# One of a round's two low weight parts moved behind the normalisation in the second attention, and the query's permutation put between transposes and value products

## The chip, the cores and the metric

The kernel runs on one core of one Trainium2 chip. The metric is the device time of the core in microseconds; the time before is 911.38 us, the median of three runs. Five engines work side by side and meet only at semaphores: PE (TensorE) multiplies matrices out of SBUF into PSUM banks, ACT (ScalarE) and DVE (VectorE) work on SBUF and PSUM, POOL (GpSimd) works on SBUF, SP issues the loads of the weights. Each engine takes its own instructions strictly in the order in which they are written.

## The reference

The network has two blocks of two kinds of layers on 256 tokens of 1024 channels; everything is float32. The part that the change touches is the last attention, layer 1 of the second block:

```python
hkv = rms_norm(x, kv_norm_g); kv = (hkv @ w_kv).reshape(B, S, 2, N_KV_HEADS, HEAD_DIM)
k_shared = rope(kv[:, :, 0], cos, sin)
kk, vv = band_blocks(k_shared), band_blocks(kv[:, :, 1])
q = rope((h @ w_q[j]).reshape(B, S, N_Q_HEADS, HEAD_DIM), cos, sin)
m = swa_sink_attention(q, kk, vv, sinks[j]) @ w_o[j]
x = x + rms_norm(m, mix_post_g[layer])
```

There are 16 query heads of 64 channels, 4 key-value heads, a causal window of 128 keys and one sink logit per head in the softmax. The rotation (`rope`) turns a pair x1, x2 of each head into x1 cos - x2 sin and x2 cos + x1 sin. A feed-forward layer with a convolution follows, and ends the program.

## The kernel before

Weights come in 268 chunks of 128 x 1024 numbers (512 KB). Each is loaded by SP into one of four raw buffers (`wraw`), and split exactly into a high and a low part of type float32r: the high part (`whi`, line 130) is a copy on ACT, the low part (`wlo`, line 140) is raw minus high, on DVE unless POOL is named. A product of a split weight with a split operand is three matmuls (line 359). Making a low part also ends the use of its raw buffer, so the load of a later chunk is written right behind each low part (`self.load()` in `low`). `W.highs(n)` writes n high parts and hands back the functions that make their low parts, so that these can be put elsewhere.

The second attention (lines 1230 to 1319) works on pairs of query heads, p0 to p7, in ten rounds of one loop, i = 0 to 9. "Round i" below is one pass of it. In the old text of the loop a round in the middle writes, in this order:

1. `scores2(i)`: eight matmuls (line 1241) into two banks; DVE reads them with mask and sink and takes the maxima (line 1252), and negates these (`nm`, line 1255).
2. `transp2(i - 1)`: six transposes of the weights `p` of the pair before (line 1275), and two copies of them to SBUF on ACT (`pT`, line 1277).
3. `pv2(i - 1)`: the products with the values (line 1285), then `split_out`: the high part `oh` on ACT (line 328) and the low part `ol` on DVE (line 329).
4. `rope_fin("q{i + 2}")`, in rounds 0 to 5: the rotation of a later query. PE multiplies the query `f` (a piece of the tile `scr`) with a permutation matrix (line 1168); DVE multiplies that with the sines (line 1170); POOL multiplies `f` with the cosines (line 1171) and adds the two (line 1172).
5. `lows`: the low parts of the chunks whose high parts the round before made. That is one in rounds 1 and 7, two in rounds 2 to 6.
6. `exps2(i)`: the exponentials on ACT (lines 1264 and 1266), which wait for `nm`; then `normalise(i)` on DVE: the sums (`sm`, line 682), their reciprocals (line 684) and four products (line 688).
7. `W.highs(2)`: up to two high parts on ACT.
8. `next(q_fill)`, in rounds 0 to 4: half a unit of the projection of query i + 3, 24 matmuls (line 359), copied to `scr` by ACT (line 1163). From round 5 on it is `wo_t0`, matmuls of the output projection.

So PE's order in a round is scores, transposes, value products, permutation, 24 matmuls. Nothing but this order and the waits on data and buffers decides when something runs. The banks for scores, value products, permutation and projection are taken from four in turn (`bank()`), five per round in rounds 1 to 4.

Of the kernel before, what the change touches and what calls it, by code (L numbers as in the profile page):

```python
# [24 lines left out]

# [1 line left out]
C_QA, C_KA, C_QB, C_KB, C_VB, C_GA, C_GB = 0, 4, 8, 12, 13, 14, 22  # L27
# [8 lines left out]

# [1 line left out]
(V_G0, V_B0, V_BOUT, V_G1, V_B1, V_BFF2, V_G2, V_B2, V_MIXPRE0, V_PSCALE, V_MIXPOST0, V_FFNPRE0,  # L38
 V_FFNPOST0, V_KVG, V_MIXPRE1, V_MIXPOST1, V_FFNPRE1, V_FFNPOST1, V_VAB, V_SINK) = range(20)

# [1 line left out]
W_POOL = 114  # L42
W_KVQ = W_POOL + 2 + 66
W_KV_AT = (0, 1, 4, 5)

# [1 line left out]
K_ID = 0  # L47
# [27 lines left out]
class Weights:  # L75
    """Streams the weight chunks: load, then an exact split w = hi + lo into two float32r parts."""

# [27 lines left out]
    def prepare(self, n=99):  # L105
        """The work on loaded chunks that goes ahead of their split."""
        while n and self.todo:
            n -= 1
            i = self.todo.pop(0)
            self.before[i](self.raw[i])  # L110
# [6 lines left out]
    def high(self):  # L117
        """The high part of the next chunk; returns what makes the low part."""
        i, r = self.split, self.raw.pop(self.split)
        while i in self.todo:  # L120
            self.prepare(1)
        slot = self.slots.pop(0)
        pool, tag = slot
        hi = pool.tile([P, 1024], F32R, tag=tag + "h", name="whi", bufs=1)
        lo = pool.tile([P, 1024], F32R, tag=tag + "l", name="wlo", bufs=1)
        for j, g in enumerate(self.gain.get(i, [])):
            d = slice(j * T, (j + 1) * T)
            self.nc.scalar.activation(out=hi[:, d], in_=r[:, d], func=AF.Identity, scale=g)
        if i not in self.gain:
            self.nc.scalar.activation(out=hi, in_=r, func=AF.Copy)  # L130
        self.ready[i] = (hi, lo, slot)
        self.split += 1

        def low(eng=None):
            for j, g in enumerate(self.gain.get(i, [])):
                d = slice(j * T, (j + 1) * T)
                self.nc.vector.scalar_tensor_tensor(out=lo[:, d], in0=r[:, d], scalar=g, in1=hi[:, d].bitcast(F32),
                                                    op0=ALU.mult, op1=ALU.subtract)
            if i not in self.gain:
                (eng or self.nc.vector).tensor_tensor(out=lo, in0=r, in1=hi.bitcast(F32), op=ALU.subtract)  # L140
            self.done += 1
            self.load()
        return low
# [4 lines left out]
    def take(self, k, c):  # L148
        """The next chunk, its two parts seen as [128, k, c]."""
        if self.taken not in self.ready:  # L150
            self.pump(1)
        hi, lo, slot = self.ready.pop(self.taken)
        self.taken += 1
        self.held.append(slot)
        return tuple(t.rearrange("p (k c) -> p k c", k=k) for t in (hi, lo)) + (slot,)
# [7 lines left out]
    def extra(self, ctx):  # L163
        """One more slot, until its pool is closed."""
        self.grow(ctx, 1)
        return self.slots[-1]
# [10 lines left out]
def model(tc, x_in, wts, bvec, cols_in, const_in, nab_in, pos_in, out):  # L177
    nc = tc.nc
    from contextlib import ExitStack
    with ExitStack() as top:  # L180
# [6 lines left out]
        def rot(pool, shape, dt, tag, name, bufs):  # L187
            """A tile of the next of bufs slots, in turn."""
            key = (id(pool), tag)
# [39 lines left out]
        class Spread:  # L229
            """A row on all partitions, in two banks."""  # L230

# [20 lines left out]

# [1 line left out]
        def rstd_of(v):  # L254
# [4 lines left out]
        def ln_rstd(st):  # L259
            """Mean and 1 / sqrt(var + eps) from the two halves' statistics."""  # L260
            mv = small([P, 2], "mv")
# [28 lines left out]
        def sq_half(src, junk, ss, q, into=None):  # L290
            """ss[:, q] = the half's sum of squares / 1024."""
            nc.scalar.activation(out=junk[:, HALF[q if into is None else into]], in_=src, func=AF.Square, scale=1.0 / 32.0,
                                 accum_out=ss[:, q:q + 1])
# [37 lines left out]
        def fm_banks(h):  # L331
            """[128 tokens, 1024] transposed into two banks."""
            bs = []
# [13 lines left out]
        def to_fm(h, xt, t):  # L347
            """Token tile t of h [128 tokens, 1024] into the split transposed operand."""
            fm_split(fm_banks(h), xt, t)
# [4 lines left out]
        def mm3(o, w, x, start, stop, w_stat):  # L354
            """o += w.x over the split parts; w_stat: the weights are the stationary operand."""
            pairs = ((0, 0), (0, 1), (1, 0))
# [4 lines left out]
        def unit_a(kx, epi, nk=8, pump=(2, None), ahead=0):  # L361
            """Two outputs [128 features, 256 tokens] of a product with stationary weights."""
            cs = [W.take(4, 256) for _ in range(nk // 4)]
# [16 lines left out]
        def unit_halves(kx, epi):  # L380
            """unit_a, one output at a time."""
            cs = [W.take(4, 256) for _ in range(2)]
# [13 lines left out]
        class Tm:  # L396
            """First units of a product with token-major outputs, so that token tile 0 can run alone."""

# [5 lines left out]
            def run(self, t, quiet=(), late=None):  # L404
                """late: what the last unit is to be followed by, emitted ahead of its last products."""
                for u in range(self.n):
# [26 lines left out]
        class Acc:  # L433
            """Token-major product accumulated over the chunks: out [256 tokens, 1024] in four banks."""

# [20 lines left out]
            def tail(self, kxs, chain0, mid, pre=0, post=3, at=(2, 2), half=lambda: None, halves=True, fills=()):  # L456
                """The last chunks: token tile 0 first, then tile 1 while chain0 runs."""
                k0 = self.nk - len(kxs)
# [21 lines left out]

# [1 line left out]
        xT = new_xt(com)  # L482
# [71 lines left out]

# [1 line left out]
        va = apool.tile([P, 2, 512], F32, name="va")  # L556
# [216 lines left out]

# [1 line left out]
        ctx_x.close()  # L775
# [22 lines left out]

# [1 line left out]
        mag = float(1.5 * 2 ** 23)  # L800
# [65 lines left out]

# [1 line left out]
        ctx_f = ExitStack()  # L868
# [43 lines left out]

# [1 line left out]
        dT = new_xt(com)  # L914
# [21 lines left out]
        def a_scale(t, r):  # L936
            """The rms factors of the tokens into the rows of the pooling matrix."""
            for a in [pa[t]] + [corner] * (t == 0):
# [9 lines left out]
        def pool_corner():  # L948
            """What the last tokens of tile 0 give to the first ones of tile 1."""
            b = bank()  # L950
# [47 lines left out]
        def resid_rms(halves, t, gpost, junk):  # L998
            """X += rms_norm(halves) * gpost."""
            ss = small([P, 2], "ss")  # L1000
# [58 lines left out]

# [1 line left out]
        def conv_ffn(layer, xt, second, gpost_row, chain_t, after, split):  # L1061
# [86 lines left out]

# [1 line left out]
        assert W.gone(extra)  # L1150
# [79 lines left out]
        def bank_ahead(n):  # L1230
            """One of the banks that the second token tile takes at the end."""
            i = (turn[id(ps), "b"] + 1 + n) % 4
# [65 lines left out]
        for i in range(10):  # L1298
            if i < 8:
                scores2(i)  # L1300
            if 1 <= i <= 8:
                transp2(i - 1)
                split_out(pv2(i - 1), *att2[i - 1])
            if i < 6:
                rope_fin(f"q{i + 2}")
            for low in lows:
                low()
            if i < 8:
                exps2(i)
                normalise(i, lambda a, j: a[:, j * P:(1 + 2 * j) * P])  # L1310
            lows = W.highs(2)
            if i == 0:
# [43 lines left out]
def fm_unit(w):  # L1356
    """[K, 256] -> chunks [128, 4 * 256]."""
    k = w.shape[0] // 128
# [3 lines left out]
def tm_chunks(w):  # L1362
    """[K, N] -> chunks of [128, 1024 / N row blocks, N]."""
    k, n = w.shape[0] // 128, w.shape[1]
# [106 lines left out]
def lay_na_bias(rpb):  # L1471
    """[8, 15, 31] -> [4, 128, 2, 384]: per query column and row parity, the offsets of six key rows."""
    flat = np.concatenate([rpb.reshape(8, -1), np.full((8, 1), NEG, np.float32)], 1)
# [35 lines left out]
```

## Time and profile before

| what | us |
|---|---|
| three runs | 908.84, 912.42, 911.38 |
| median | 911.38 |
| span of the profiled execution, first to last instruction | 908.3 |
| second attention, loop rounds 1 to 8, first transpose to last `oh` | 638.6 to 692.8 |
| PE, DVE, ACT, POOL busy over the span | 859.9, 631.5, 493.0, 242.6 |

No time of the profiled execution is known besides its span; the shortest of the three runs is 0.5 us above it. Busy times say how long an engine held instructions, and what bounds a stretch is read from the waits in that stretch. A wait in a timeline stands in brackets, with the engine and the tile that ended it. PE's ends are modelled, so the place where the next PE instruction starts is the better mark.

### The profile page before, as it was taken

To read this page: it belongs to the slowest core of one execution; us is meant where nothing else is said; L and a number is where in the kernel's file an instruction comes from. 1 tells how busy PE (TensorE), PEld (TensorE's weight loads), DVE (VectorE), ACT (ScalarE), POOL (GpSimd) and SP (SyncE) were. 2 spreads that over 40 slices of the span, in tenths; PEclk is the share of its full clock that TensorE was granted. 3 is DMA by queue.
4 is the path that set the end of the run, shared out by engine and by line. 5 is a ranking of instruction groups with operands and counts; after the bars stand their busy time and mean duration, and the time that the engine had idled before them with its cause. 6 is when DMAs were issued, how large, how long until landed. Compare 5 with 4: busy or idle time off the path is not lost.

```text
span 908.3 us, 15197 instructions
## 1 busy us (share of the span) xinstructions
PE 859.9 (95%) x5872; PEld 771.2 (85%) x5872; DVE 631.5 (70%) x1019; ACT 493.0 (54%) x905; POOL 242.6 (27%) x196
## 2 busy tenths in 40 slices
PE   6999999889899999989999999999889899999997
PEld 5988899779698999779999999989666898999995
DVE  5466754877738755777789777665786678977762
ACT  4555755433526645354657545555775466754551
POOL 4161040324998000353240000138631223000000
PEclk9999999989899999999999999999999999999999
DMA  8683354346526855623547555433252454755431
GB/s 307 203 275 125 117 186 138 118 136 233 193 94 217 294 187 186 208 71 115 186 152 248 205 200 172 162 119 125 94 155 101 141 184 166 253 208 187 174 127 46
DMA packets 43897, 154.61 MB, mean 170 GB/s; under 512 B 5009, under 2 KB 5905, under 8 KB 43826
## 3 DMA queue, kind: packets, MB, share of 16 engines
q1 hardware_dynamic: 41616, 146.90, 47.8%
q0 software_dynamic: 1632, 5.93, 2.0%
q8 instruction: 46, 0.75, 0.3%
q10 hardware_dynamic: 578, 0.82, 0.3%
q14 instruction: 25, 0.20, 0.1%
HBM read 152.58 MB, written 1.05 MB: 169 GB/s over the span
## 4 chain that ended last, share of the span: by engine, by line
PE 68%; DVE 12%; issue 6%; ACT 5%; DMA 5%; POOL 2%; SPq 0%; DVEq 0%; POOLq 0%; ACTq 0%
PE bank_a L359 35%; PE bank_b L359 22%; PE bank_a L414 5%; DVE wlo L140 4%; DMA wraw<-wts_dram 3%; ACT whi L130 2%; DMA nab<-nab_dram 1%; PE bank_a L1285 1%; PE bank_a L710 1%; POOL wlo L140 1%; PE bank_b L699 1%; DVE X L321 1%; PE bank_b L647 1%; DMA v<-bvec_dram 1%; POOL wraw L845 1%
## 5 line engine op out<-in xcount | busy, mean ns | idle before, releaser
L140 DVE TENSOR_TENSOR wlo<-wraw,whi 128x1024 fp32r<-128x1024 f32 x225 | 288.8, 1313 | 81.2 <-ACT whi L130 75.2
L359 PE MATMUL bank_a<-xh,whi 128*128 128x256 f32 x1056 | 299.6, 284 | 5.0 <-DVE cv L1075 5.0
L359 PE MATMUL bank_a<-xh,wlo 128*128 128x256 f32 x1056 | 296.1, 280 | 0.8 <-POOL wlo L140 0.4
L359 PE MATMUL bank_a<-xl,whi 128*128 128x256 f32 x1056 | 295.9, 280 | 0.0
L130 ACT ACTIVATE whi<-wraw 128x1024 fp32r<-128x1024 f32 x261 | 265.1, 1049 | 40.3 <-DMA wraw<-wts_dram 33.9
L359 PEld LDWEIGHTS bank_a<-xh,whi 128*128 128x128 f32 x1056 | 199.3, 189 | 10.2 <-ACT whi L130 6.5
L359 PEld LDWEIGHTS bank_a<-xl,whi 128*128 128x128 f32 x1056 | 199.4, 189 | 1.9
L359 PEld LDWEIGHTS bank_a<-xh,wlo 128*128 128x128 f32 x1056 | 199.3, 189 | 1.4 <-DVE wlo L140 0.8
L140 POOL TENSOR_TENSOR wlo<-wraw,whi 128x1024 fp32r<-128x1024 f32 x36 | 93.6, 2613 | 175.6 <-ACT whi L130 87.5
L1072 ACT ACTIVATE cv<-bank_a,cols 128x256 f32<-128x256 f32 x76 | 41.9, 558 | 85.7 <-PE bank_a L359 85.7
L256 POOL TENSOR_TENSOR rstd<-ve,neghalf 128x1 f32<-128x1 f32 x22 | 13.4, 611 | 233.8 <-DVE ve L297 192.1
L1073 DVE SCALAR_TENSOR_TENSOR cv<-bank_a,cols,cv 128x255 f32<-128x255 f32 x76 | 36.5, 481 | 50.2 <-ACT cv L1072 49.9
L359 PE MATMUL bank_b<-wlo,ah 128*128 128x512 f32 x176 | 69.5, 395 | 0.0
L359 PE MATMUL bank_b<-whi,al 128*128 128x512 f32 x176 | 69.3, 394 | 0.0
L359 PE MATMUL bank_b<-whi,ah 128*128 128x512 f32 x176 | 69.3, 394 | 0.0
L856 POOL TENSOR_SCALAR wraw<-wraw,cols 128x256 f32<-128x256 f32 x28 | 30.2, 1094 | 125.9 <-DMA wraw<-wts_dram 122.7
L359 PE MATMUL bank_b<-whi,uh 128*128 128x512 f32 x128 | 51.5, 402 | 4.3 <-ACT uh L328 4.3
L359 PE MATMUL bank_b<-whi,ul 128*128 128x512 f32 x128 | 51.5, 402 | 1.7 <-DVE ul L329 1.7
L359 PE MATMUL bank_b<-wlo,uh 128*128 128x512 f32 x128 | 51.5, 402 | 0.0
L359 PEld LDWEIGHTS bank_b<-wlo,ah 128*128 128x128 f32 x176 | 33.1, 188 | 7.6
L359 PEld LDWEIGHTS bank_b<-whi,ah 128*128 128x128 f32 x176 | 33.1, 188 | 6.3
L1075 DVE SCALAR_TENSOR_TENSOR cv<-bank_a,cols,cv 128x254 f32<-128x254 f32 x76 | 36.6, 482 | 2.7
(201 smaller groups left out, 1371.3 us busy)
## 6 DMA issues: line engine op xcount, KB each, us to landing
wraw<-wts_dram SPq DMA_DIRECT2D x268, 512.0 KB, 4.5
v<-bvec_dram POOLq DMA_DIRECT2D x10, 512.0 KB, 6.7
v<-bvec_dram SPq DMA_DIRECT2D x4, 512.0 KB, 7.1
nab<-nab_dram SPq DMA_DIRECT2D x4, 384.0 KB, 6.3
poolA<-const_dram POOLq DMA_DIRECT2D x1, 544.0 KB, 6.1
scr<-x_dram SPq DMA_DIRECT2D x2, 256.0 KB, 3.1
scr<-x_dram SPq DMA_DIRECT2D x1, 512.0 KB, 10.3
out_dram<-X SPq DMA_DIRECT2D x2, 256.0 KB, 2.1
```

The costliest lines, as they stand in the source:

```text
L130: self.nc.scalar.activation(out=hi, in_=r, func=AF.Copy)
L140: (eng or self.nc.vector).tensor_tensor(out=lo, in0=r, in1=hi.bitcast(F32), op=ALU.subtract)
L256: nc.gpsimd.tensor_tensor(out=r, in0=v, in1=neghalf, op=ALU.pow)
L321: nc.vector.scalar_tensor_tensor(out=x[:, s], in0=junk[:, s], scalar=r, in1=x[:, s], op0=ALU.mult, op1=ALU.add)
L359: nc.tensor.matmul(o, lhsT=l, rhs=r, start=start and i == 0, stop=stop and i == 2)
L414: nc.tensor.matmul(o[:, :256], lhsT=self.kx(k)[b][:, t * P:(t + 1) * P], rhs=self.cs[u][k // 4][a][:, k % 4, :], start=i == 0 and k == 0, ...
L647: nc.tensor.matmul(s[e][:, j * T:(j + 1) * T], lhsT=q[r, j * P:(j + 1) * P], rhs=k[r, :], start=True, stop=True)
L699: nc.tensor.transpose(out=b[:, s * T + j * P:s * T + (j + 1) * P], in_=pt[e][:, j, s * P:(s + 1) * P], identity=ident)
L856: nc.gpsimd.tensor_scalar(out=d, in0=d, scalar1=g, scalar2=None, op0=ALU.mult)
L1072: nc.scalar.activation(out=v, in_=o[:, :T], func=AF.Identity, scale=col(c + 2), bias=col(c + 3))
L1073: nc.vector.scalar_tensor_tensor(out=v[:, 1:T], in0=o[:, 0:T - 1], scalar=col(c + 1), in1=v[:, 1:T], op0=ALU.mult, op1=ALU.add)
L1075: nc.vector.scalar_tensor_tensor(out=v[:, 2:T], in0=o[:, 0:T - 2], scalar=col(c), in1=v[:, 2:T], op0=ALU.mult, op1=ALU.add)
```

## The change

In the loop of the second attention two things are written in another place. The permutation of a query (`rope_fin`) now stands between the transposes and the value products of a round. And of a round's low parts the first stays ahead of the exponentials and the normalisation, while the second, where there is one, comes behind them. The rest of the diff takes comments and docstrings away.

```diff
             if 1 <= i <= 8:
                 transp2(i - 1)
-                split_out(pv2(i - 1), *att2[i - 1])
             if i < 6:
                 rope_fin(f"q{i + 2}")
-            for low in lows:
+            if 1 <= i <= 8:
+                split_out(pv2(i - 1), *att2[i - 1])
+            for low in lows[:1]:
                 low()
             if i < 8:
                 exps2(i)
                 normalise(i, lambda a, j: a[:, j * P:(1 + 2 * j) * P])
+            for low in lows[1:]:
+                low()
             lows = W.highs(2)
```

On PE, in round 2 (rows with + are new there, rows with - are gone; `bank_t` takes the transposes):

```order
 L1241 MATMUL bank_a<-k_6876,q_6894 128x256 x2
 L1275 MATMUL bank_t<-ident,p 128x128 x6
+L1168 MATMUL bank_a<-scr,perm_6631 128x256
 L1285 MATMUL bank_a<-pT,v_6635 64x256 x2
 L1285 MATMUL bank_a<-pT,v_6635 64x128 x2
-L1168 MATMUL bank_a<-scr,perm_6631 128x256
 L359 MATMUL bank_a<-xh,whi 128x256
 L359 MATMUL bank_a<-xl,whi 128x256
```

The permutation moved from behind the value products to ahead of them; rounds 1 to 5 have this. On DVE, in round 3 before, from the negated maxima to the first score operation of the next round:

```order
L1255 TENSOR_SCALAR nm<-mx 128x4
L329 TENSOR_TENSOR ol<-bank_a,oh 128x256
L1170 TENSOR_TENSOR q_7232<-bank_a,sin_2272 128x256
L140 TENSOR_TENSOR wlo<-wraw,whi 128x1024 x2
L682 TENSOR_TENSOR sm<-sm,es 128x4
L684 RECIPROCAL rc<-sm 128x4
L688 TENSOR_SCALAR p<-p,rc 128x128
L688 TENSOR_SCALAR p<-p,rc 128x256
L688 TENSOR_SCALAR p<-p,rc 128x128
L688 TENSOR_SCALAR p<-p,rc 128x256
L1252 ISA p,mx<-bank_a,l1m,sink 128x128
```

And the same stretch of DVE after:

```order
L1255 TENSOR_SCALAR nm<-mx 128x4
L1170 TENSOR_TENSOR q_7223<-bank_a,sin_2272 128x256
L329 TENSOR_TENSOR ol<-bank_a,oh 128x256
L140 TENSOR_TENSOR wlo<-wraw,whi 128x1024
L682 TENSOR_TENSOR sm<-sm,es 128x4
L684 RECIPROCAL rc<-sm 128x4
L688 TENSOR_SCALAR p<-p,rc 128x128
L688 TENSOR_SCALAR p<-p,rc 128x256
L688 TENSOR_SCALAR p<-p,rc 128x128
L688 TENSOR_SCALAR p<-p,rc 128x256
L140 TENSOR_TENSOR wlo<-wraw,whi 128x1024
L1252 ISA p,mx<-bank_a,l1m,sink 128x128
```

The sine product went ahead of `ol`, and one low part behind the normalisation, ahead of the next round's score operations. Rounds 2 to 6 have the second; the order of ACT, POOL and SP is the same in both, but SP's load behind the second low part now waits for it in its new place.

## Rows read from the trace of the kernel before

**Rows 1.** Chain of waits, 646 to 693 us, shares by line.

```profile
by line: DVE wlo L140 26.3%; PE bank_a L1285 17.9%; PE bank_t L1275 10.1%; ACT pT L1277 8.5%; PE bank_b L359 7.7%; DVE p L688 6.4%; issue 5.3%; ACT oh L328 4.1%; ACT p L1264 3.7%; DVE q L1170 2.7%; DVE ol L329 2.4%; DVE rc L684 2.0%; PE ban
```

**Rows 2.** Windows, one round each: length; PE, PEld, DVE, ACT, POOL busy; clock.

```profile
646.30:654.18 7.88, 7.01 (x50) 5.11 (x49) 6.87 (x19) 6.07 (x18) 2.93 (x3) 1.00 0.23 62
654.18:661.79 7.61, 6.84 (x49) 5.18 (x49) 6.61 (x20) 5.62 (x16) 2.35 (x2) 1.00 0.47 142
669.39:677.38 7.99, 6.96 (x37) 4.46 (x37) 6.71 (x20) 5.38 (x15) 3.46 (x4) 1.00 0.44 139
677.38:683.85 6.47, 6.22 (x35) 4.04 (x35) 5.47 (x19) 4.41 (x14) 0.00 (x0) 1.00 0.89 298
683.85:689.85 6.00, 5.37 (x27) 3.52 (x27) 4.43 (x18) 3.46 (x13) 0.00 (x0) 1.00 0.45 157
```

**Rows 3.** Timeline of PE: start, duration (us), instruction, count, idle time before it.

```profile
646.30 0.55 PE L1275 MATMUL bank_t<-ident,p 128*128 128x128 f32 x3
...
654.18 1.16 PE L1275 MATMUL bank_t<-ident,p 128*128 128x128 f32 x6 [0.64 <-DVE p L688]
...
655.52 1.32 PE L1285 MATMUL bank_a<-pT,v 128*64 128x256 f32 x8 [0.18 <-ACT pT L1277]
...
656.77 0.70 PE L1168 MATMUL bank_a<-scr,perm 128*128 128x256 f32 x2
...
657.12 0.47 PE L359 MATMUL bank_a<-xh,whi 128*128 128x256 f32 x1
...
660.28 0.93 PE L1241 MATMUL bank_a<-k,q 64*128 64x128 f32 x8
```

**Rows 4.** Timeline of DVE, round 3, and two rows from other rounds.

```profile
645.00 2.23 DVE L688 TENSOR_SCALAR p<-p,rc 128x128 f32<-128x128 f32 x4
...
654.76 0.35 DVE L1252 CUSTOM_DVE_ANT_0 p<-bank_a,l1m,sink 128x128 f32<-128x128 f32 x1
...
656.23 0.17 DVE L1255 TENSOR_SCALAR nm<-mx 128x4 f32<-128x4 f32 x1
...
657.30 0.42 DVE L329 TENSOR_TENSOR ol<-bank_a,oh 128x256 fp32r<-128x256 f32 x1 [0.90 <-ACT oh L328]
...
657.97 3.16 DVE L140 TENSOR_TENSOR wlo<-wraw,whi 128x1024 fp32r<-128x1024 f32 x2
...
661.05 0.15 DVE L682 TENSOR_TENSOR sm<-sm,es 128x4 f32<-128x4 f32 x1
...
661.45 1.01 DVE L688 TENSOR_SCALAR p<-p,rc 128x128 f32<-128x128 f32 x4
...
680.74 2.35 DVE L140 TENSOR_TENSOR wlo<-wraw,whi 128x1024 fp32r<-128x1024 f32 x2
```

**Rows 5.** Timeline of POOL, a rotary add alone, and one beside two lows.

```profile
631.07 0.74 POOL L1172 TENSOR_TENSOR q<-q,scr 128x256 f32<-128x256 f32 x1
...
658.44 1.60 POOL L1172 TENSOR_TENSOR q<-q,scr 128x256 f32<-128x256 f32 x1
```

**Rows 6.** Timeline of ACT, round 3 to the next.

```profile
656.88 0.38 ACT L328 ACTIVATE oh<-bank_a 128x256 fp32r<-128x256 f32 x1 [0.95 <-PE bank_a L1285]
...
657.16 0.39 ACT L1264 ACTIVATE p<-p,nm 128x128 f32<-128x128 f32 x1
...
659.29 1.99 ACT L130 ACTIVATE whi<-wraw 128x1024 fp32r<-128x1024 f32 x2
...
661.19 0.36 ACT L1163 ACTIVATE scr<-bank_a 128x256 f32<-128x256 f32 x1
...
662.58 0.95 ACT L1277 ACTIVATE pT<-bank_t 128x384 f32<-128x384 f32 x2 [1.03 <-PE bank_t L1275]
...
664.49 0.38 ACT L328 ACTIVATE oh<-bank_a 128x256 fp32r<-128x256 f32 x1 [0.95 <-PE bank_a L1285]
```

**Rows 7.** DMA issues, 630 to 712 us: count, KB each, us to landing.

```profile
wraw<-wts_dram SPq DMA_DIRECT2D x18, 512.0 KB, 3.7
v<-bvec_dram POOLq DMA_DIRECT2D x2, 512.0 KB, 6.8
```

## The prediction

> **What bounds the kernel now.** I read the chain of waits of the second attention first [rows 1]: the low parts on DVE are its largest item, 26.3%, ahead of the value products on PE (17.9%) and the transposes (10.1%), so DVE's order in a round sets PE's pace. The windows [rows 2], each from a round's first transpose to the next round's, show rounds of 7.88, 7.61 and 7.99 us with POOL at work (a further one of 7.60 lies between), then 6.47 and 6.00 once POOL is idle. The granted clock is 1.00, the upper of its two levels (2.4 GHz), throughout.
>
> PE's timeline [rows 3] has two stalls per round: 0.64 us for the first normalised weights (DVE's `p`), 0.18 us for the first copy `pT`. DVE [rows 4] shows why. It idles 0.90 us until `oh` comes, because `ol` stands first; then come `ol`, the sine product and both lows, and only then the sums: 657.30 to 661.05. The exponentials were done at 659.29, when ACT began its high parts [rows 6]: the normalisation stands 1.76 us behind its data. A second thing sits inside that: two lows alone take 2.35 us, here 3.16 [rows 4], and POOL's rotary add takes 1.60 beside them, 0.74 alone [rows 5].
>
> The Trainium skill (SBUF — State Buffer, section Who interferes with whom) explains the last rows by a pair of ports that DVE and POOL lock against each other for a whole instruction, whoever starts first; two SBUF inputs take it, one PSUM input does not. The rows agree: 3.16 - 2.35 = 0.81 is lost on one side and 0.86 on the other, and `ol` keeps its 0.42. By that rule alone nothing is saved by merely shifting POOL's add, since the first low would wait it out (up to 0.74); by stretching in proportion it would lose less. Neither changes the sum below, where that low has slack, but the rule makes the fourth rival.
>
> **The second low behind the normalisation** (rounds 2 to 6, five instructions moved, none added). DVE's way from `ol` to the sums loses one low, about 1.2 us (half of 2.35), and then ends with the exponentials. The sums start about 1.8 us sooner against their round. What is late next must be found by adding up each engine's loop, with the permutation already ahead.
>
> - PE: transposes 0.55 for three [rows 3], that is about 0.8 for six when nothing paces them (now 1.16, since `p` comes piece by piece over 1.01); permutation 0.35 (657.12 - 656.77); value products 1.25 (656.77 - 655.52); 24 matmuls 3.16 (660.28 - 657.12); scores 0.86 to 0.93. Sum 6.4 to 6.5.
> - ACT [rows 6]: `oh` 0.28 (to 657.16), exponentials 2.13, two highs 1.90, `scr` up to 0.36, two copies 0.95, and 0.96 from the copies' end (663.53) to the next `oh` (664.49). Sum 6.5 to 6.6.
> - DVE, as a loop with ACT: exponentials 2.13, sums and reciprocals 0.40, four products 1.01, the second low 1.17, score operations 1.47 (656.23 - 654.76), `nm` 0.17, and the exponentials again. With 0.1 of handing over, 6.4 to 6.5.
>
> All three lie within 0.2 us of each other, at about 6.5 against 7.61. That is the gain of a regular round, 1.1 us, and it leaves no cover: each tenth that any of the three loses is a tenth of the round. The lower bound of a round is PE's sum without the copies' pacing, 6.2; the upper is 7.0, if hand-overs and POOL put 0.5 on the DVE loop. I take 6.5, which the undisturbed round of 6.47 also shows possible [rows 2].
>
> **The permutation ahead of the value products** (rounds 1 to 5, one PE instruction pair, one DVE product and, through them, two POOL instructions). On PE it fills 0.35 us in which the copies `pT` run: the wait of 0.18 goes, and the value products find both copies ready sooner. `scr`, which it reads, must be there: in the new steady round ACT makes it just ahead of the copies, so it does not come later than they do. `oh` would come up to 0.17 later; the wait that goes pays for it. On DVE the sine product slides into the 0.90 us in which DVE waits for `oh`, at no cost. POOL's cosine product (0.74) then falls beside the score operations, which read PSUM, and its add ahead of the first low instead of between the two lows. I cost a late add at 0.5 us on the first low, hidden because the exponentials end later than that low. It is already contained in the 6.5; alone, this move would give some 0.2 to 0.3 per round on PE.
>
> **The load behind the second low** starts about 0.8 us later in its round (sums 1.76 sooner, but sums, products and the low itself, 0.40 + 1.01 + 1.17, now ahead of it) while the rounds get shorter. It is wanted by the second high of the next round, which comes after score operations, `nm`, exponentials and one high: 1.47 + 0.17 + 2.13 + 0.95, with 0.1 of handing over 4.8 us. Landing takes 3.7 [rows 7]: cover of 1.1 us, and no cost.
>
> **The sum**, round by round. Round 1 has one low and POOL is busy with earlier work, so it keeps its time. Round 2's window, 7.88, gets 6.8, since its `p` (2.23, beside POOL [rows 4]) still hold its transposes: -1.1. Two rounds of 7.61 and 7.60 get 6.5: -2.2. The round of 7.99 has the permutation but half of an output projection (PE 3.08) in place of the 24 matmuls, no `scr`, and the next has no copy pending: 6.4, -1.6. The round of 6.47 loses only what paces its transposes, -0.3 (from 0 to -0.4). The last, 6.00, waited for nothing but `oh` and the exponentials; now the second low ahead of its score operations holds `nm` back: +0.3 (0 to +0.4). Total -4.9, by bounds: regular rounds at 6.2 would give -5.8 (three times 0.3 more), at 7.0 -2.5 (rival 1). I take 0.2 off for hand-overs at three equal loops: -4.7. What follows the attention starts from its last value products: the shift is handed on whole, because the later loads are written behind later lows and shift too.
>
> The profiled execution is known by its span, 908.3 us; the run nearest to it took 908.84, the median 911.38 lies 3.1 above the span. Nothing in the edit scales with that, so I subtract from the median: 911.4 - 4.7 = 906.7 us.
>
> **Rivals.**
>
> 1. *DVE becomes the bound.* The score operations now stand behind a low; with 0.5 us of hand-overs and POOL's add, rounds last 7.0 (the first of them 7.3), the round of 7.99 gets 6.9, and the last two lose 0.4 together: -0.6 x 3 - 1.1 + 0.4 = -2.5, 908.9 us. For it: DVE's loop has 0.1 of slack. Against it: DVE is busy only 6.61 of 7.61, 0.81 of that being time lost beside POOL.
> 2. *The second load comes late.* At 6.0 us rather than 3.7 the second high waits 1.2, and `scr`, the permutation and `pT` behind it on ACT. Rounds 3 to 5 have such a high: 3.6 given back, 910.3 us. For it: the vector loads, which run beside the weights, take 6.8 for 512 KB [rows 7]. Against it: loads in these rounds come singly now, and less than half of the DMA time is used in three of the windows.
> 3. *Taken back later.* The feed-forward after the attention waits for a load; if that ended on something that does not move, 911.4 us. Against it: that load is written behind a low part which waits for this attention's end.
> 4. *Slower: POOL locks the normalisation.* If POOL's add comes after the first low has begun, it waits for the low and then falls on the four products, which take 2.23 instead of 1.01 beside POOL [rows 4]. The place is the DVE loop; each low there can meet a POOL product too, at the 0.6 that the second of a pair loses at most (3.16 - 2.35 = 0.81 over both): 6.5 + 1.2 + 0.6 + 0.6 = 8.9 per round against 7.88, 7.61, 7.60 and 7.99 (+1.0, +1.3, +1.3, +0.9), and +0.8 in the last two rounds: +5.3, 916.7 us. It decides from the point where the sine product comes later than `oh`; by the timeline `nm` ends 0.5 us before `oh` begins (656.40, 656.88). The Trainium skill's rule of the lock, named above, would put POOL's add there.
> 5. *More than forecast.* With both copies ready the value products run their two halves side by side, the rounds come to 6.2: -5.8, 905.6 us. For it: PE's loop is the shortest of the three. Against it: ACT's 6.5 then still holds.
>
> That the change doesn't do what it says is excluded by the order of instructions, but for round 1.
>
> **How the numbers follow.** Chances: forecast 0.60, rivals 0.14, 0.05, 0.05, 0.07 and 0.09. A measurement of this kernel tells 0.5%, 4.6 us, from no change, and the forecast of -4.7 sits on that bound. It holds 0.38 of its 0.60 for faster, with rival 5: 0.47. Within 0.5%: the forecast's other 0.22, rivals 1 to 3, 0.02 of rival 4: 0.48. Slower: the other 0.05 of rival 4. The likeliest case alone is 905.4 to 908.0; the range takes in rivals 1, 2 and 5 and the runs' own scatter of about a microsecond: 904.0 to 910.3.
>
> **What would show it.** Right: rounds from transpose to transpose of 6.4 to 6.6; no PE wait for `p` in rounds 3 to 6; DVE's sums right behind the exponentials' end; the sine product ahead of `ol`, inside the wait for `oh`; POOL's add back near 0.74 and the first low below 1.8 us; ACT as the engine without idle time. Wrong: a wait of the second high for its load (rival 2), exponentials waiting for `nm` in regular rounds (rival 1), products of over 2 us (rival 4), or a longer wait for weights in the feed-forward.

## The result, and the profile after

The changed kernel takes 906.65 us, the median of eight runs (903.89 to 907.66), against 911.31 us for the kernel before, eight runs (908.84 to 917.01) beside it. The ratio is 0.9948, with an interval of 95% from 0.9929 to 0.9967: faster, by 4.7 us or 0.5%, and on which side of 0.5% the interval leaves open. The forecast was 906.7 us, 4.7 less than the median of three runs that was known then.

The profiled execution of the changed kernel took 905.71 us. Its page begins:

```profile
span 903.9 us, 15201 instructions
...
PE 855.5 (95%) x5872; PEld 770.0 (85%) x5872; DVE 632.4 (70%) x1019; ACT 492.1 (54%) x905; POOL 238.7 (26%) x196
```

The span is 4.4 us shorter than before. Every run of the changed kernel is listed 1.8 us above its span (905.71 and 903.9), so the span of 908.3 us before answers to some 910.1 us, an estimate, and not to the run of 908.84 us that the prediction took as the nearest. Comparing the same instructions in both traces: the first transposes of round 1 start 0.94 us later than before (639.50 against 638.56), with nothing changed ahead of them; then 5.1 us are won between the first transposes of round 2 and those of round 8; what comes after is shifted as a whole (the last transposes by -4.11, the last instruction by -4.4). The start of round 1 lies anywhere from 635.9 to 639.9 us in the ten traces of this case. So the stretch "round 2 to round 8" is used below as the measure: 43.54 us before, 38.47 after. It is read from one execution each, but rounds 3 and 4 agree within 0.01 us in both traces (7.61 and 7.60, 6.42 twice).

The windows of the changed kernel, one round each, from first transpose to first transpose (columns: length; PE, PEld, DVE, ACT and POOL busy, with counts; granted clock; DMA share; GB/s):

```profile
647.26:653.97 6.71, 6.43 (x50) 5.02 (x48) 5.74 (x20) 5.11 (x17) 2.07 (x3) 1.00 0.17 45
653.97:660.39 6.42, 6.31 (x50) 5.11 (x48) 6.30 (x20) 5.47 (x17) 1.47 (x2) 1.00 0.55 166
666.81:673.26 6.45, 6.34 (x39) 4.36 (x37) 6.32 (x20) 5.50 (x17) 2.59 (x4) 1.00 0.56 204
673.26:679.46 6.20, 5.89 (x36) 4.04 (x34) 5.34 (x18) 5.09 (x15) 0.00 (x0) 1.00 0.88 311
679.46:685.73 6.27, 5.15 (x28) 3.53 (x27) 5.32 (x18) 3.50 (x13) 0.00 (x0) 1.00 0.51 164
```

These answer to [rows 2], line by line: 7.88, 7.61, 7.99, 6.47 and 6.00 became 6.71, 6.42, 6.45, 6.20 and 6.27. (The round from 660.39, not shown, is another one of 6.42.) The clock was at its upper level in both.

PE in round 3 (start, duration in us, instruction, count; idle time before it would stand in brackets), against [rows 3]:

```profile
653.97 0.87 PE L1275 MATMUL bank_t<-ident,p 128*128 128x128 f32 x6
654.96 0.70 PE L1168 MATMUL bank_a<-scr,perm 128*128 128x256 f32 x2
655.59 0.98 PE L1285 MATMUL bank_a<-pT,v 128*64 128x256 f32 x8
...
660.39 0.87 PE L1275 MATMUL bank_t<-ident,p 128*128 128x128 f32 x6
```

No wait stands in brackets here: the 0.64 us for `p` and the 0.18 us for `pT` are gone, six transposes take 0.87 instead of 1.16 since each piece of `p` lies ready when it is wanted, and the value products 0.98 instead of 1.32. PE is not free of ACT, though. The loads of its weights (PEld), which go ahead of the matmuls, wait for `scr` and for the copies `pT`:

```profile
654.96 0.30 PEld L1168 LDWEIGHTS bank_a<-scr,perm 128*128 128x128 f32 x2 [0.35 <-ACT scr L1163]
655.59 0.74 PEld L1285 LDWEIGHTS bank_a<-pT,v 128*64 128x64 f32 x8 [0.33 <-ACT pT L1277]
```

DVE in the same round, against [rows 4]:

```profile
656.71 0.17 DVE L1255 TENSOR_SCALAR nm<-mx 128x4 f32<-128x4 f32 x1
656.79 0.42 DVE L1170 TENSOR_TENSOR q<-bank_a,sin 128x256 f32<-128x256 f32 x1
657.13 0.41 DVE L329 TENSOR_TENSOR ol<-bank_a,oh 128x256 fp32r<-128x256 f32 x1
657.46 1.72 DVE L140 TENSOR_TENSOR wlo<-wraw,whi 128x1024 fp32r<-128x1024 f32 x1
659.19 0.16 DVE L682 TENSOR_TENSOR sm<-sm,es 128x4 f32<-128x4 f32 x1
...
659.60 1.01 DVE L688 TENSOR_SCALAR p<-p,rc 128x128 f32<-128x128 f32 x4
660.53 1.22 DVE L140 TENSOR_TENSOR wlo<-wraw,whi 128x1024 fp32r<-128x1024 f32 x1
661.66 0.34 DVE L1252 CUSTOM_DVE_ANT_0 p<-bank_a,l1m,sink 128x128 f32<-128x128 f32 x1
...
663.13 0.17 DVE L1255 TENSOR_SCALAR nm<-mx 128x4 f32<-128x4 f32 x1
```

From `nm` on DVE has no gap. The 0.90 us in which it had idled for `oh` are gone: the second low now stands ahead of the score operations, so `nm` ends at 656.88, when `oh` (656.61, below) is already running. The sine product and `ol` follow, and the sums come at 659.19. One low is 1.72 us long, the other, behind the products, 1.22. POOL's add, against [rows 5], is back at its time alone, and ACT, against [rows 6], has ended its exponentials 0.1 us ahead of the sums:

```profile
655.74 0.73 POOL L1171 TENSOR_TENSOR scr<-scr,cos 128x256 f32<-128x256 f32 x1 [4.56 <-PE bank_a L1168]
657.35 0.74 POOL L1172 TENSOR_TENSOR q<-q,scr 128x256 f32<-128x256 f32 x1 [0.88 <-DVE q L1170]
```

```profile
656.61 0.39 ACT L328 ACTIVATE oh<-bank_a 128x256 fp32r<-128x256 f32 x1 [0.95 <-PE bank_a L1285]
656.92 0.41 ACT L1264 ACTIVATE p<-p,nm 128x128 f32<-128x128 f32 x1
...
659.06 1.99 ACT L130 ACTIVATE whi<-wraw 128x1024 fp32r<-128x1024 f32 x2
660.96 0.36 ACT L1163 ACTIVATE scr<-bank_a 128x256 f32<-128x256 f32 x1
...
663.02 0.38 ACT L328 ACTIVATE oh<-bank_a 128x256 fp32r<-128x256 f32 x1 [0.95 <-PE bank_a L1285]
663.34 0.40 ACT L1264 ACTIVATE p<-p,nm 128x128 f32<-128x128 f32 x1
```

The sums had stood 1.76 us behind the exponentials. The second high (659.06, two in one row) waits for no load. In the chain of waits (shares by line, 647 to 690 us) the lows have fallen from the first place, 26.3% [rows 1], to 5.3%. The exponentials lead, and value products, high parts and permutation, which follow them by way of ACT and PE, hold 12.2, 11.6 and 5.9%:

```profile
by line: ACT p L1264 25.2%; PE bank_a L1285 12.2%; ACT whi L130 11.6%; DVE p L688 8.9%; DVE p L1252 6.1%; PE bank_a L1168 5.9%; DVE wlo L140 5.3%; ACT es L1266 5.3%; PE bank_b L359 4.3%; issue 3.8%; ACT oh L328 3.6%; PE bank_t L1275 2.9%; A
```

### The profile page after: what moved, and what is told of

It reads as the page before. It is cut to its first block, busy times and chain, and to the rows that moved or that the text cites. A ratio compares the mean times of both kernels' runs of the same rounds, so it can differ in the third digit from the quotient of the medians.

```text
span 903.9 us, 15201 instructions
## 1 busy us (share of the span) xinstructions
PE 855.5 (95%) x5872; PEld 770.0 (85%) x5872; DVE 632.4 (70%) x1019; ACT 492.1 (54%) x905; POOL 238.7 (26%) x196
## 3 DMA queue, kind: packets, MB, share of 16 engines
HBM read 152.58 MB, written 1.05 MB: 170 GB/s over the span
## 4 chain that ended last, share of the span: by engine, by line
PE 68%; DVE 10%; issue 8%; ACT 6%; DMA 5%; POOL 3%; SPq 0%; POOLq 0%; DVEq 0%; ACTq 0%
PE bank_a L359 36%; PE bank_b L359 22%; PE bank_a L414 4%; DMA wraw<-wts_dram 3%; DVE wlo L140 3%; ACT whi L130 2%; POOL wlo L140 2%; ACT p L1264 2%; PE bank_a L710 1%; PE bank_b L699 1%; DVE X L321 1%; DMA v<-bvec_dram 1%; PE bank_b L647 1%; DMA nab<-nab_dram 1%; DVE p L688 1%
```

## The experiments

Each kernel's result is given as the lengths of its rounds, from the first transposes of round 2 on, and their sum. "Rounds" are those of 7.88, 7.61, 7.60, 7.99, 6.47 and 6.00 us in the kernel before (43.54) and of 6.71, 6.42, 6.42, 6.45, 6.20 and 6.27 in the changed one (38.47). Edits are shown against the changed kernel, unless said otherwise. Ratios are to the kernel before; where none is given, one execution was read. The intervals of most of these ratios overlap, so the shares rest on the rounds, from one execution of each kernel; rounds that an edit leaves alone come out the same within 0.01 us (6.47 and 5.99 or 6.00 in four of the kernels). Theory A, the prediction's own, books most of the gain on the second low.

**The permutation alone.** Both lows back ahead of the normalisation.

```diff
-            for low in lows[:1]:
+            for low in lows:
                 low()
...
-            for low in lows[1:]:
-                low()
```

> The permutation between transposes and value products as in the changed kernel, both low parts ahead of the normalisation as before. Measure: from the first transposes of round 2 to those of round 8, 43.55 us before, 38.47 us changed. Theory A (the prediction's shares): the second low behind the normalisation is what pays, the permutation alone gives 0.2 to 0.3 us a round on PE: 42.4 to 42.8 us, regular rounds 7.3 to 7.4, time 0.1% under before. Theory B (either part alone pays nearly all): the permutation alone takes POOL's add from between the lows (0.8 us) and the sine product from behind oh (0.4 us), so the sums stand 0.5 instead of 1.8 us behind the exponentials, which PE's own work covers: 38.3 to 39.2 us, regular rounds 6.5 to 6.6, time ratio to before about 0.995.

Rounds of 6.87, 6.53, 6.51, 6.75, 6.47 and 5.99: 39.12 us, 4.4 of the 5.1 us. The time is 907.11 us, ratio 0.9959 [0.9942, 0.9976]. Theory A falls. DVE and POOL in round 3 of it (columns as above):

```profile
655.79 0.41 DVE L1170 TENSOR_TENSOR q<-bank_a,sin 128x256 f32<-128x256 f32 x1
656.55 0.42 DVE L329 TENSOR_TENSOR ol<-bank_a,oh 128x256 fp32r<-128x256 f32 x1 [0.35 <-ACT oh L328]
656.89 2.41 DVE L140 TENSOR_TENSOR wlo<-wraw,whi 128x1024 fp32r<-128x1024 f32 x2
```

```profile
656.34 0.74 POOL L1172 TENSOR_TENSOR q<-q,scr 128x256 f32<-128x256 f32 x1 [0.49 <-DVE q L1170]
```

The sine product fills part of DVE's wait for `oh`, the add follows right behind it and is over (657.08) 0.2 us after the lows begin, and the pair of lows takes 2.41 us instead of 3.16.

**The second low alone.** The permutation back behind the value products.

```diff
+            if 1 <= i <= 8:
+                split_out(pv2(i - 1), *att2[i - 1])
             if i < 6:
                 rope_fin(f"q{i + 2}")
-            if 1 <= i <= 8:
-                split_out(pv2(i - 1), *att2[i - 1])
```

> The second low part behind the normalisation as in the changed kernel, the permutation behind the value products as before. Same measure. Theory A: 39.3 to 39.8 us, that is the changed kernel's 38.47 plus what the permutation gave on PE. Theory B: 38.8 to 39.3 us, regular rounds 6.6 to 6.75; so the two parts' gains would not add up (each about 4.5 us alone, 5.1 together). Theory C (the second low in the loop from exponentials over scores to exponentials costs what it saves unless the sine product goes ahead): 42 us or more.

Rounds of 7.14, 6.70, 6.69, 6.87, 6.19 and 6.33: 39.93 us, 3.6 us won. The time is 908.47 us, ratio 0.9952 [0.9931, 0.9973]. That is just above theory A's 39.8, 0.6 above theory B's range and well under theory C's 42. With the first experiment: 4.4 and 3.6 alone, 5.1 together, so the gains don't add up, and each part by itself takes most of what DVE's late sums cost. What is left differs. With the permutation alone PE's own work sets the round: it is busy 6.47 of 6.52 us, and the chain of waits runs on PE without a break from 653.53 to 673.31. With the second low alone it is DVE and ACT. POOL's add begins after the first low here (658.21, 1.48 us long), runs on when that is over, and holds the sums back, which take 0.39, 0.45 and 0.65 us in rounds 3 to 5 instead of 0.16. That is the prediction's fourth rival on a small scale:

```profile
658.68 1.60 POOL L1172 TENSOR_TENSOR q<-q,scr 128x256 f32<-128x256 f32 x1
```

```profile
659.91 0.39 DVE L682 TENSOR_TENSOR sm<-sm,es 128x4 f32<-128x4 f32 x1 [0.23 <-ACT es L1266]
```

**PE's order alone.** The permutation is early on PE, but DVE's order is the old one, `oh`'s low part ahead of the sine product, and both lows ahead of the normalisation.

```diff
-            if i < 6:
-                rope_fin(f"q{i + 2}")
+            rest = rope_fin(f"q{i + 2}", True) if i < 6 else None
             if 1 <= i <= 8:
                 split_out(pv2(i - 1), *att2[i - 1])
+            if rest:
+                rest()
...
```

(`rope_fin` with True writes the permutation on PE and hands back what writes the rest, DVE's and POOL's products. The low parts are edited as in the first experiment.)

> The permutation on PE between transposes and value products, but DVE's sine product behind oh's low part and both lows ahead of the normalisation, so that only PE's order is new and DVE's is the old one. Same measure; permutation with the sine product alone gave 39.12, old 43.55. If the gain of the moved permutation comes from PE's order (0.35 us of work under the copies), 0.3 a round: 42 to 42.6 us with POOL's add still beside the lows at 1.6 us. If most comes from PE after all, 39 to 40 us.

Rounds of 7.70, 7.35, 7.35, 7.63, 6.47 and 5.99: 42.49 us, 1.05 us won. DVE and POOL:

```profile
661.75 0.42 DVE L329 TENSOR_TENSOR ol<-bank_a,oh 128x256 fp32r<-128x256 f32 x1 [0.69 <-ACT oh L328]
662.09 0.41 DVE L1175 TENSOR_TENSOR q<-bank_a,sin 128x256 f32<-128x256 f32 x1
662.42 2.89 DVE L140 TENSOR_TENSOR wlo<-wraw,whi 128x1024 fp32r<-128x1024 f32 x2
```

```profile
662.65 1.58 POOL L1177 TENSOR_TENSOR q<-q,scr 128x256 f32<-128x256 f32 x1 [1.61 <-DVE q L1175]
```

DVE waits 0.69 us for `oh` again, and the add (1.58) again begins beside the lows (2.89 for the pair). So of the 4.4 us that the moved permutation is worth, PE's order gives 1.05, from 0.18 to 0.36 in each of the four rounds that have it, and DVE's and POOL's order, which follows from it, gives the other 3.4. In a regular round that is 0.83 us (7.35 to 6.52): 0.34 since the sine product no longer stands between `ol` and the lows, and 0.48 since the pair of lows is shorter (2.89 to 2.41).

**The old order without POOL's two products** in the rounds. The queries q2 to q7 then have the sine product alone. The edit is against the kernel before.

```diff
-                nc.gpsimd.tensor_tensor(out=f, in0=f, in1=cos2, op=ALU.mult)
-                nc.gpsimd.tensor_tensor(out=q, in0=q, in1=f, op=ALU.add)
+                if name in ("k0", "k1", "q0", "q1"):
+                    nc.gpsimd.tensor_tensor(out=f, in0=f, in1=cos2, op=ALU.mult)
+                    nc.gpsimd.tensor_tensor(out=q, in0=q, in1=f, op=ALU.add)
```

> The old order of the loop, with POOL's two products for the queries q2 to q7 left out (these queries get the sine product alone; the result is another one). Same measure. If the lock between POOL's add and the two lows is a large part of the old round (0.81 us of 7.61), regular rounds fall to 6.7 to 6.8 us and the whole to 39 to 39.5 us, without either part of the change. If the lock only fills time in which DVE would have waited, 7.4 to 7.6 us remain and 42.5 to 43.5 us.

Rounds of 6.65, 6.85, 6.80, 6.78, 6.47 and 5.99: 39.54 us, 4.0 us won without either part of the change. The pair of lows takes 2.35 us, and DVE still idles for `oh`:

```profile
661.62 0.43 DVE L329 TENSOR_TENSOR ol<-bank_a,oh 128x256 fp32r<-128x256 f32 x1 [0.90 <-ACT oh L328]
...
662.29 2.35 DVE L140 TENSOR_TENSOR wlo<-wraw,whi 128x1024 fp32r<-128x1024 f32 x2
```

So the collision of POOL's products with DVE was most of what the old rounds lost: 0.8 us in each regular round, as much as the pair of lows gets shorter (3.16 to 2.35), and 1.2 us each in round 2, where part of the normalisation stands beside POOL too, and in the round of 7.99, where the lows account for 0.8 and the rest was not traced.

**The new order without POOL's two products**, by the same edit.

> The changed kernel with POOL's two products for the queries q2 to q7 left out (they get the sine product alone; the result is another one). Measure: from the first transposes of round 2 to those of round 8, 38.47 us changed. If in the new order POOL's add only takes time from the first low that the exponentials cover, nothing is won: 38.0 to 38.5 us, regular rounds 6.35 to 6.45; the first low falls from 1.72 to 1.2 us and DVE then waits some 0.5 us for the exponentials. If DVE's work alone sets the round (it has no gap in rounds 3 to 5), each round loses the 0.55 us of the lock: 5.9 us rounds, about 36 us.

Rounds of 6.24, 6.39, 6.39, 6.37, 6.21 and 6.31: 37.91 us. Regular rounds win 0.03; most of the rest is round 2's (6.71 to 6.24), whose four products take 1.01 us here and 2.26 beside POOL in the changed kernel. In the windows DVE is now busy 5.78 of 6.40 us instead of 6.30 of 6.42:

```profile
651.90:658.30 6.40, 6.33 (x51) 5.12 (x49) 5.78 (x20) 5.45 (x17) 0.00 (x0) 1.00 0.51 173
```

```profile
661.76 1.21 DVE L140 TENSOR_TENSOR wlo<-wraw,whi 128x1024 fp32r<-128x1024 f32 x1
663.49 0.16 DVE L682 TENSOR_TENSOR sm<-sm,es 128x4 f32<-128x4 f32 x1 [0.52 <-ACT es L1267]
```

The first low is 1.21 us long instead of 1.72, and DVE then waits 0.52 us for the exponentials. An engine without a gap was not the bound. With POOL's products gone, the old and the new order still differ by 1.6 us (39.54 and 37.91), so 1.6 of the 5.1 us that the change wins don't need that collision, and 3.4 do.

**Both lows behind the normalisation** (round 1's one low stays ahead).

```diff
-            for low in lows[:1]:
+            for low in (lows if i == 1 else []):
                 low()
...
-            for low in lows[1:]:
+            for low in (lows if i > 1 else []):
                 low()
```

> As the changed kernel, but from round 2 on both low parts come behind the normalisation (round 1's one low stays ahead). Same measure. If the loop exponentials - sums - products - low - score operations - negated maxima - exponentials on ACT and DVE sets the changed kernel's round (6.42 us, DVE without a gap), one more low in it costs its 1.15 us: regular rounds 7.4 to 7.6 us, 43 to 44 us in all, no gain left against before. If ACT's own loop (copies, oh, exponentials, highs) or PE sets it, the low's place costs nothing until DVE is full: 6.4 to 6.6 us rounds, 38.5 to 39.5 us.

Rounds of 6.71, 7.38, 7.55, 7.36, 7.55 and 7.55: 44.10 us. The time is 912.35 us, ratio 1.0008 [0.9992, 1.0025]: nothing is left of the gain. DVE, and ACT's exponentials:

```profile
668.25 0.16 DVE L682 TENSOR_TENSOR sm<-sm,es 128x4 f32<-128x4 f32 x1 [1.64 <-ACT es L1266]
...
671.85 0.35 DVE L1252 CUSTOM_DVE_ANT_0 p<-bank_a,l1m,sink 128x128 f32<-128x128 f32 x1
...
673.32 0.17 DVE L1255 TENSOR_SCALAR nm<-mx 128x4 f32<-128x4 f32 x1
...
675.79 0.16 DVE L682 TENSOR_TENSOR sm<-sm,es 128x4 f32<-128x4 f32 x1 [1.64 <-ACT es L1266]
```

```profile
673.52 0.40 ACT L1264 ACTIVATE p<-p,nm 128x128 f32<-128x128 f32 x1 [1.04 <-DVE nm L1255]
```

From sums (668.25) to sums (675.79) is 7.54 us. The exponentials wait 1.04 us for `nm`, since the score operations (671.85) stand behind two lows, and the sums then wait 1.64 us for the exponentials. A low more in the loop costs 7.54 - 6.42 = 1.12 us a round, about its own length. So the loop exponentials, sums, products, low, score operations, `nm` has next to no cover in the changed kernel: what lengthens it lengthens the round. That a shorter one would shorten the round doesn't follow from this.

**POOL's add twice** in the new order.

```diff
                 nc.gpsimd.tensor_tensor(out=q, in0=q, in1=f, op=ALU.add)
+                if name not in ("k0", "k1", "q0", "q1"):
+                    nc.gpsimd.tensor_tensor(out=rot(ap, [P, T], F32, "again", "again", 2), in0=q, in1=f, op=ALU.add)
```

> The changed kernel with POOL's add of the rotation done twice in the rounds, the second time into a tile that nobody reads. Same measure. This is the prediction's fourth rival made on purpose: POOL work that comes after the first low has begun. If the lock goes to whoever waits, the second add runs behind the first low and falls on the sums and products of the normalisation: products of 1.6 to 1.8 us instead of 1.01, regular rounds 6.9 to 7.2 us, 40.5 to 42 us in all. If it runs straight behind the first add, the low waits 0.74 more and the sums with it: also about 7.1 us. If there is slack left, 6.4 to 6.6 us, 38.5 to 39.2.

Rounds of 6.64, 6.50, 6.97, 6.80, 6.36 and 6.41: 39.68 us, 1.2 more than the changed kernel and less than expected. POOL and DVE in the round from 657.17:

```profile
660.91 0.73 POOL L1172 TENSOR_TENSOR q<-q,scr 128x256 f32<-128x256 f32 x1 [0.71 <-DVE q L1170]
661.73 1.60 POOL L1174 TENSOR_TENSOR again<-q,scr 128x256 f32<-128x256 f32 x1
```

```profile
661.10 1.63 DVE L140 TENSOR_TENSOR wlo<-wraw,whi 128x1024 fp32r<-128x1024 f32 x1
662.88 0.47 DVE L682 TENSOR_TENSOR sm<-sm,es 128x4 f32<-128x4 f32 x1 [0.15 <-ACT es L1268]
...
663.59 1.01 DVE L688 TENSOR_SCALAR p<-p,rc 128x128 f32<-128x128 f32 x4
```

The low (661.10) waits for the first add, the second add (661.73) waits for the low, runs when that is over and stops the sums: an instruction on 128 x 4 numbers takes 0.47 us here and 0.61 us in the next round instead of 0.16. The products keep their 1.01 us. So POOL work that comes late does push the normalisation back, by up to 0.5 us in a round.

**The second low on POOL**, in rounds 3 to 6, ahead of the rotation's products.

```diff
+            early = lows[1:] if i >= 3 else []
+            for low in early:
+                low(nc.gpsimd, 1)
             if i < 6:
                 rope_fin(f"q{i + 2}")
...
+            for low in early:
+                low(None, 2)
...
-            for low in lows[1:]:
+            for low in ([] if early else lows[1:]):
                 low()
```

(The 1 makes the low part without the load that follows it, the 2 writes that load alone, behind the first low.)

> The changed kernel with the second low part of rounds 3 to 6 made by POOL, ahead of the rotation's products (2.6 us there, against 1.15 on DVE), its load behind it. Same measure. DVE's loop gets 1.15 us shorter, so that ACT and PE are left as bounds: 6.3 to 6.45 us a round, the round of 6.27 back to 5.75 to 6.0, 37.7 to 38.3 us in all, 0.2 to 0.8 better than the changed kernel, which the time can't tell. If POOL's low meets the first low or the products on the shared ports, rounds of 7 us and more, 41 us.

Rounds of 6.72, 6.75, 6.77, 6.59, 6.55 and 6.00: 39.37 us; the time is 907.16 us, ratio 0.9957 [0.9935, 0.9978]. Neither expectation holds: regular rounds are longer by 0.3 than in the changed kernel, though DVE's loop lost a low. DVE and POOL:

```profile
660.02 2.37 POOL L140 TENSOR_TENSOR wlo<-wraw,whi 128x1024 fp32r<-128x1024 f32 x1 [1.87 <-ACT whi L130]
```

```profile
660.88 1.53 DVE L1256 TENSOR_SCALAR nm<-mx 128x4 f32<-128x4 f32 x1
...
664.72 0.16 DVE L683 TENSOR_TENSOR sm<-sm,es 128x4 f32<-128x4 f32 x1 [0.52 <-ACT es L1267]
```

POOL's low misses the first low and the products, as it was meant to, but `nm`, four numbers per partition, takes 1.53 us instead of 0.17: it begins while the low runs and ends with it (662.41 and 662.39), and the exponentials begin 0.54 us behind `oh` instead of 0.31. A new loop has come about: exponentials, two highs, POOL's low, which waits 1.87 us for the second of them, `nm`, and the exponentials again, 6.64 us from sums to sums (658.08 to 664.72) against 6.42. So this run doesn't show what the DVE loop without its low is worth.

No version tried that computes the same is better than the changed kernel; the one without POOL's products, 0.6 us shorter, computes something else.

## Why the prediction was right

The time was met to 0.1 us, and the sum it came from was met round by round. Predicted against measured: round 2's window 6.8 and 6.71, the regular ones 6.5 and 6.42, the next 6.4 and 6.45, then 6.2 and 6.20, and 6.3 and 6.27. In all -4.9 was worked out, and -5.1 is in the trace.

- *What bounds a round.* Right for the old kernel: sums 1.76 us behind their data, and POOL's add beside the lows. The experiment without POOL's products puts 4.0 us on that collision, by itself.
- *Three loops within 0.2 us of each other.* Right, and closer than it says. In the changed kernel's rows the loop of DVE and ACT runs 656.92 (exponentials), 659.19, 659.60, 660.53, 661.66, 663.13, 663.34, which is 6.42, and one low more in it costs 1.1 us a round. The loop of ACT and PE is all but as long: exponentials 656.92, highs 659.06, `scr` 660.96, permutation 661.37, value products 662.00, `oh` 663.02. Where nothing else holds them the exponentials begin 0.28 us behind `oh` (as in the kernel before); here it is 0.31 and 0.32, so `nm` holds a round for 0.04 us at most, and ACT and PE would give some 6.38 without it, an estimate from these rows. A shorter DVE loop alone had nearly nothing left to win; the experiments show that it has no cover, not that it is the only bound. PE's sum came out (6.42), but not its parts: 0.99, 0.63, 0.91, 3.04 and 0.85 us against 0.8, 0.35, 1.25, 3.16 and up to 0.93, since the value products are quicker and the waits for `scr` and `pT` were not in it.
- *The permutation "alone, ... some 0.2 to 0.3 per round on PE".* Right for PE (0.25 and 0.26 in the regular rounds), but this step mis-sized the move: with DVE's and POOL's order, which it also changes, it is worth 4.4 us alone. The prediction had both effects in its text, the sine product in the idle 0.90 us and the add off the lows, and booked them as free or as already contained in the second low's gain. As the second low alone is worth 3.6, the total was right and the shares were not: given the permutation, the second low adds 0.65 us (39.12 to 38.47), given the second low, the permutation adds 1.46.
- *The second low ahead of the last rounds' score operations costs 0.3.* Right: 6.00 became 6.27, with ACT waiting 0.29 us for `nm` there. In the round before it won 0.27.
- *The load behind the second low is covered.* Right here, no high of these rounds waits for a load. With both lows behind, one such wait of 0.30 us shows, so that rival's mechanism exists.
- *"ACT as the engine without idle time".* Wrong: ACT idles 0.95 us per round for the value products, and DVE is the engine without a gap. The prediction's own sum for ACT had this wait in it, 0.96 us. Idle time told nothing of the bound, as the kernel without POOL's products shows.
- *The fourth rival*, POOL locking the normalisation, did not occur in the changed kernel, by 0.11 us: POOL's add begins at 657.35, the first low at 657.46. The sine product had come later than `oh` (656.79, 656.61), which the prediction named as the deciding point; `ol`, which stands between it and the low, made the difference. Made on purpose the rival cost 1.2 us in all, not 5, and in the kernel with the second low alone at most 1.5: the products were not stretched, only the sums were held, once a round.
- *0.2 us off for hand-overs* was not needed in the rounds. That the time came out at the forecast is in part luck: the medians scatter by more than that (911.38, 911.31 and 910.97 for the kernel before).

## What to carry to other kernels

Where two edits shorten the same wait, work out each one alone: their gains are not shares of a sum, and here either gave most of it. When an instruction is moved on one engine, follow those on the other engines that hang on it, since the moved matmul itself was worth 1.05 us and the add that it set free on POOL the larger part of the rest (0.48 of 0.83 us in a regular round). And look for the bound as a loop through several engines, from an instruction to the same one a round later, and not as the engine without gaps; where two loops tie, shortening one wins nothing.

## What the runs showed of the hardware

In the rows shown, the DVE instructions that read SBUF alone (lows, sums, `nm`, products) and POOL's products and lows lengthened each other as if one ran behind the other, and a small DVE instruction was not safe: `nm` on 128 x 4 took 1.53 us instead of 0.17 beside a POOL low of 2.37, and the sums 0.61 instead of 0.16. So the order of the instructions and the waits on data and buffers are not all that decides when something runs. It is no rule for every pair: in the trace of before the reciprocal, on 128 x 4 of SBUF too, kept its 0.18 us inside a POOL add (644.79), and `nm` its 0.17 inside one of POOL's scalings of weights (635.15). The Trainium skill (SBUF — State Buffer, section Who interferes with whom) names the forms that take the shared ports, and the traces agree in the pairs shown here. The score operations, which read PSUM and the mask in SBUF, kept their 0.35 and 0.48 us beside POOL's cosine product, and `ol` and the sine product, which read PSUM too, kept theirs in every row shown. A low part that POOL makes in place of DVE thus cost DVE 1.36 us on `nm`, more than the 1.15 us that it spared, where this small instruction of the loop fell into its 2.4 us.

Six transposes took 0.87 us with each piece of their data ready in time, 1.16 us when DVE's four products, 1.01 us long, ended one after the other under them; and the value products took 0.98 us where the second copy ended 0.06 us after they began, 1.32 where it ended 0.41 after. A single transpose lasts 0.27 to 0.33 us in both; they start further apart. A dependency that arrives in pieces thus lengthens what the profile counts as busy, and not only the waits.
